# Two transformer blocks on one core: 38 of block 1's 56 input units computed as 19 pairs in seven half-size products each, with results through DRAM and the FFN's weight sums moved later

## The chip, the cores and the metric

The kernel runs on one core of a Trainium2 chip. The metric is the device time of one execution, in microseconds (us). The engines are TensorE (PE, matmuls; PEld is its weight load), VectorE (DVE), ScalarE (ACT), GpSimd (POOL) and SyncE (SP), which issues every DMA of this kernel from one in-order queue. Sixteen DMA engines move the data.

## What is computed

Two blocks on a sequence of 1024 rows of 1024 float32 numbers. Cut to what the change touches, block 1 is

```
h = rms_norm(x)
v_c, b_c, c_c, z_c, q, k, v, z_a, gate_a, gate_b = split(h @ w_in)     # 1024 columns each; k, v 256
y_c = b_c * conv3(c_c * v_c) * silu(z_c)          # causal depthwise convolution over the sequence
y_a = y_c @ w_conv_out
o   = sliding_window_attention(q, k, v, sinks) * silu(z_a)             # window 128, 16 heads of 64
y_b = o @ w_attn_out
x1  = x + (sigmoid(gate_a) * y_a + sigmoid(gate_b) * y_b) @ w_out
```

Block 2 is full causal attention with forget gates, a layer norm, a gated FFN of width 2816 with a convolution, a second layer norm and a gated embedding. It is not changed, but the sums of its FFN weights are made early, within block 1.

## The kernel before

All products keep float32 accuracy with three passes: an operand x is split into `hi` (ACT, line 84 or 81) and `lo` = x - hi (DVE, line 88 or 90), and each product is hi*hi + hi*lo + lo*hi. Operands that move through PE lie as two halves of 512 sequence positions (`XT.mov`). A *unit* is 128 output columns: a weight tile of 1024 x 128 (0.5 MB, rows of 512 bytes in DRAM, loaded by `spec_unit`, line 157) against both halves, 2 x 8 x 3 = 48 matmuls of 128x512 (`gemm_ws`, lines 181 to 183). `WQ` holds the list of weight tiles: `get` hands out one that is split, loads two ahead (`fetch`) and splits one ahead.

Block 1 goes in this order:

- `weave`: `attn1_stream` (32 items of the sliding attention, five stages in a software pipeline) and `beside` (8 convolution tiles of four input units each in `conv_stream`, then 3 units of gate b) take turns by an estimate of their matmul time, with the share RATIO = 0.68. The 16 tile buffers of h (`hT`) feed both. Results go to DRAM (`yc_d`, `o_d`, `gb_d`).
- `gates_b`: 5 more units of gate b; y_c comes back from DRAM and is split into `ycT`.
- `y_a`: 8 times a unit of gate a and a unit of w_conv_out. `z_a`: 8 units of z_a, times o from DRAM, into `ozT`. `y_b`: 8 units of w_attn_out, merged with gate b and y_a into `mT`. `w_out`: two halves of 512 columns; the first matmul group of a half needs all four weight tiles of that half.

All 56 *input units* (32 of the convolution, 16 gates, 8 z_a) are plain units with `hT`.

The FFN of block 2 is already computed by seven products of half size in place of eight (19 column tiles of the up projection, and the down projection). Its sums of weight blocks are made in block 1 by `Sums`, called `early`: each `early.step()` forms the sums of the pair loaded one call ago (four POOL additions of 128x512, line 381), stores them (four DMAs of 0.25 MB, `us_d` or `t_d`) and loads the next pair (two DMAs of 0.5 MB). There are 30 pairs, 19 of w_up (512-byte rows) and 11 of w_down. A call stands in 5 units of `gates_b`, in each of the 16 units of `y_a`, the 8 of `z_a` and the 8 of `y_b`.

`X7` and `up_products` are that FFN scheme: `X7.build` forms four combinations of quarter blocks of the moving operand, each with hi and lo; seven products of 12 matmuls accumulate in PSUM and are combined by ACT copies and DVE additions. Tiles of 4 KB per partition come from one pool of 46 buffers, tiles of 2 KB from a pool of 8, and there are 8 PSUM banks. The order on each engine is set by a scheduler at build time; the listings below show what it made. SP issues in its order, and a store waits there for its data, with every later DMA behind it.

Of the kernel before, what the change touches and what calls it, by code (L numbers as in the profile page):

```python
# [14 lines left out]
RATIO = 0.68  # L15
NG = 3
# [40 lines left out]
def tile_two_blocks(ctx: ExitStack, tc: tile.TileContext, I, out, dbg=None):  # L57
# [18 lines left out]
    def f(ap):  # L76
        return ap.bitcast(F32)
# [153 lines left out]
    for c in range(8):
        wq.add(spec_unit(w_in, C_G + c * 128))
        wq.add(spec_unit(I["w_conv_out"][0], c * 128))
    for c in range(8):
        wq.add(spec_unit(w_in, C_ZA + c * 128))
    for c in range(8):
        wq.add(spec_unit(I["w_attn_out"][0], c * 128))
    for ch in range(2):
        for kp in range(4):
            wq.add(spec_rows(I["w_out"][0], 2 * kp, 2, ch * 512, 512))  # L240
# [10 lines left out]
    add_v(0)  # L251
    for j in range(8):
        wq.add(spec_unit(w2i, j * 128))
        wq.add(spec_unit(w2i, 1024 + j * 128))
        if j % 2 == 1 and j < 7:
            add_v(j // 2 + 1)
    for ch in range(2):
        for kp in range(4):
# [107 lines left out]
    o_d = dr.tile([8, 128, 1024], F32, name="o_d")  # L366
    gb_d = dr.tile([8, 128, 1024], F32, name="gb_d")
# [64 lines left out]

    def conv_stream():
        for ct in range(8):
# [28 lines left out]
            cw = [pv1[:, 8 + 8 * k + ct:9 + 8 * k + ct] for k in range(3)]  # L463
            y = t4(name="y")
            dve.tensor_scalar(y, up, cw[2], None, op0=OP.mult)
            dve.scalar_tensor_tensor(out=y[:, 1:], in0=up[:, :1023], scalar=cw[1], in1=y[:, 1:],
                                     op0=OP.mult, op1=OP.add)
            dve.scalar_tensor_tensor(out=y[:, 2:], in0=up[:, :1022], scalar=cw[0], in1=y[:, 2:],
                                     op0=OP.mult, op1=OP.add)
# [174 lines left out]
    def yc_back(c):  # L644
        yr = t4(name="yr")
        sp.dma_start(out=yr, in_=yc_d[c])
        for hf in range(2):
            split_half(ycT, c, hf, yr[:, HS[hf]])

    def gates_b(c0, c1, back):  # L650
        for c in range(c0, c1):
            w = wq.get()
            if c >= NG:
                early.step()
            gt = t4(name="gt")
            for b in back(c):
                yc_back(b)
# [3 lines left out]
            sp.dma_start(out=gb_d[c], in_=gt)  # L661

    def y_a():
        for c in range(8):
            w = wq.get()
            early.step()
            gt = t4(name="gt")
            for hf in range(2):
                ps = yield from gemm_ws(w, hT, hf)
                act.activation(gt[:, HS[hf]], ps, AF.Sigmoid, bias=pv1[:, 32 + c:33 + c])  # L670
            w = wq.get()
            early.step()
            for hf in range(2):
# [4 lines left out]
    def z_a():  # L678
        for c in range(8):
            w = wq.get()  # L680
            early.step()
            orr = t4(name="orr")
            sp.dma_start(out=orr, in_=o_d[c])
            for hf in range(2):
                ps = yield from gemm_ws(w, hT, hf)
                s = t2(name="sz")
                act.activation(s, ps, AF.Silu)
                dve.tensor_tensor(out=s, in0=s, in1=orr[:, HS[hf]], op=OP.mult)
                split_half(ozT, c, hf, s)
# [488 lines left out]

# [3 lines left out]

    class X7:

        def __init__(self, x):
            self.x, self.T = x, {}  # L1190

        def build(self, kp, e=dve):
            b11, b21 = self.x.pair(0, kp), self.x.pair(0, 2 + kp)
            b12, b22 = self.x.pair(1, kp), self.x.pair(1, 2 + kp)

            def less(out, a, b):

                if isinstance(b, tuple):
                    tmp = t4((128, 2, 512), name="xs")
                    tt(e, tmp, f(a[1]), f(b[1]), OP.subtract)  # L1200
                    tt(e, out, f(a[0]), f(b[0]), OP.subtract)
                else:
                    tmp = f(a[1])
                    tt(e, out, f(a[0]), b, OP.subtract)
                tt(e, out, out, tmp, OP.add)

            def parts(i, src):
                h, l = t4((128, 2, 512), F32R, "xsh"), t4((128, 2, 512), F32R, "xsl")
                hi(h, src)
                lo(l, src, h)  # L1210
                self.T[i, kp] = h, l

            xt = {}
            for i, a, b in ((5, b12, b11), (6, b22, 5), (7, b22, b12), (4, b21, 6)):
                xt[i] = t4((128, 2, 512), name=f"xt{i}")
                less(xt[i], a, b if isinstance(b, tuple) else xt[b])
                yield
                parts(i, xt[i])
                yield

        def mov(self, i, q):
            if i in (1, 2, 3):
                return self.x.mov(q + (i > 1) * 4, int(i == 3))
            h, l = self.T[i, q // 2]
            return h[:, q % 2, :], l[:, q % 2, :]
# [39 lines left out]
    def product(ps, w, i, more=False):  # L1265
        for q in range(4):
            xh, xl = x7.mov(i, q)
            c = slice(q * 128, q * 128 + 128)
            st = q == 0 and not more
            pe.matmul(ps, lhsT=w[0][:, c], rhs=xh, start=st, stop=False, skip_group_check=more)  # L1270
            pe.matmul(ps, lhsT=w[0][:, c], rhs=xl, start=False, stop=False, skip_group_check=more)  # L1271
            pe.matmul(ps, lhsT=w[1][:, c], rhs=xh, start=False, stop=q == 3, skip_group_check=more)  # L1272

    def up_products(ct, gs, u):
        ps = {}

        def go(i, on=None):
            if i in (1, 6, 7, 4):
                op_split()
            if on is None:  # L1280
                ps[i] = bank()
            product(ps[on or i], ops.pop((ct, i)), i, more=on is not None)

        go(1)
        u1 = y2("u1")
        act.activation(u1, ps[1], AF.Copy)
        go(2)
        tt(dve, gs[:, HS[0]], ps[2], u1, OP.add)
        go(6, on=1)
        u2 = y2("u2")  # L1290
        act.activation(u2, ps[1], AF.Copy)
        go(5)
        u4 = y2("u4")
        tt(dve, u4, ps[5], u2, OP.add)
        go(7)
        tt(dve, u[:, HS[1]], ps[7], u4, OP.add)
        go(3)
        tt(dve, gs[:, HS[1]], ps[3], u4, OP.add)
        go(4, on=7)
        tt(dve, u[:, HS[0]], ps[7], u2, OP.add)  # L1300
# [264 lines left out]
```

## Time and profile before

| | us |
|---|---|
| median of 3 runs (lowest, highest) | 2537.41 (2536.05, 2537.45) |
| the profiled execution | 2536.48 |
| its span, first to last instruction | 2534.7 |
| PE busy | 2480.9 |
| DVE busy | 1457.0 |
| ACT busy | 1032.0 |
| POOL busy | 495.5 |

The terms of a sum are to be read against the profiled execution. Busy PE time is modelled up to the next matmul, so a gap in it is a wait of PE, while the share alone says little about the rate.

### The profile page before, as it was taken

To read this page: it belongs to the slowest core of one execution; us is meant where nothing else is said; L and a number is where in the kernel's file an instruction comes from. 1 tells how busy PE (TensorE), PEld (TensorE's weight loads), DVE (VectorE), ACT (ScalarE), POOL (GpSimd) and SP (SyncE) were. 2 spreads that over 40 slices of the span, in tenths; PEclk is the share of its full clock that TensorE was granted. 3 is DMA by queue.
4 is the path that set the end of the run, shared out by engine and by line. 5 is a ranking of instruction groups with operands and counts; after the bars stand their busy time and mean duration, and the time that the engine had idled before them with its cause. 6 is when DMAs were issued, how large, how long until landed. Compare 5 with 4: busy or idle time off the path is not lost. (4 is left out here: it accounts for less than half of the span.)

```text
span 2534.7 us, 33819 instructions
## 1 busy us (share of the span) xinstructions
PE 2480.9 (98%) x12558; PEld 2115.9 (83%) x12558; DVE 1457.0 (57%) x2859; ACT 1032.0 (41%) x1947; POOL 495.5 (20%) x446
## 2 busy tenths in 40 slices
PE   8999999999999999999999999999799999999999
PEld 7888888888888888888989898887677877888887
DVE  5566666755321355334666656568756566676873
ACT  4354444546221232124655656652333333354321
POOL 2000000000355561002232333414000000000331
PEclk9999999999999999999999999999999999999999
DMA  5121121212899997231111112523244444587512
GB/s 166 42 59 51 38 63 52 59 42 70 271 279 270 296 327 247 88 118 55 53 57 43 51 55 75 179 70 102 59 131 142 137 150 128 180 311 255 189 67 84
DMA packets 282480, 323.83 MB, mean 128 GB/s; under 512 B 23746, under 2 KB 197834, under 8 KB 282314
## 3 DMA queue, kind: packets, MB, share of 16 engines
q1 hardware_dynamic: 282314, 321.66, 39.3%
q8 instruction: 99, 1.62, 0.3%
q14 instruction: 67, 0.55, 0.1%
HBM read 233.20 MB, written 88.41 MB: 127 GB/s over the span
## 5 line engine op out<-in xcount | busy, mean ns | idle before, releaser
L181 PE MATMUL ps<-hTh,wh 128*128 128x512 f32 x896 | 353.0, 394 | 2.6 <-DVE hTl L90 2.5
L183 PE MATMUL ps<-hTh,wl 128*128 128x512 f32 x896 | 351.1, 392 | 0.0
L182 PE MATMUL ps<-hTl,wh 128*128 128x512 f32 x896 | 350.7, 391 | 0.0
L88 DVE TENSOR_TENSOR wl<-wraw,wh 128x1024 fp32r<-128x1024 f32 (+1 forms) x115 | 143.6, 1258 | 177.7 <-ACT wh L84 91.5
L84 ACT ACTIVATE wh<-wraw 128x1024 fp32r<-128x1024 f32 (+2 forms) x143 | 145.1, 1027 | 137.3 <-DMA us_d<-wraw 36.9
L183 PEld LDWEIGHTS ps<-hTh,wl 128*128 128x128 f32 x896 | 168.1, 188 | 35.7
L181 PEld LDWEIGHTS ps<-hTh,wh 128*128 128x128 f32 x896 | 168.4, 188 | 31.9 <-DVE hTl L90 3.1
L182 PEld LDWEIGHTS ps<-hTl,wh 128*128 128x128 f32 x896 | 168.4, 188 | 29.0
L1122 POOL TENSOR_SCALAR sm<-sm 128x1 f32<-128x1 f32 x16 | 11.6, 725 | 680.7 <-DVE sm L1120 680.7
L381 POOL TENSOR_TENSOR wraw<-wraw 128x512 f32<-128x512 f32 x76 | 105.8, 1393 | 162.2 <-DMA wraw<-in_ffn_w_up_dram 121.5
L1431 PE MATMUL ps<-dl,dh 128*128 128x512 f32 x308 | 119.9, 389 | 1.7 <-DVE dl L88 1.7
L1432 PE MATMUL ps<-dh,dl 128*128 128x512 f32 x308 | 119.9, 389 | 0.0
L88 POOL TENSOR_TENSOR wl<-wraw,wh 128x1024 fp32r<-128x1024 f32 (+2 forms) x28 | 65.1, 2331 | 267.1 <-ACT wh L84 245.1
L1430 PE MATMUL ps<-dh 128*128 128x512 f32 x308 | 117.1, 390 | 0.0
L88 DVE TENSOR_TENSOR phl<-ps,phl 128x512 fp32r<-128x512 f32 (+1 forms) x160 | 97.4, 633 | 31.6 <-ACT phl L84 30.3
L88 DVE TENSOR_TENSOR dl<-dr,dh 128x1024 fp32r<-128x1024 f32 x77 | 93.0, 1222 | 36.1 <-ACT dh L84 25.8
L321 POOL TENSOR_SCALAR sm<-sm 128x5 f32<-128x5 f32 (+1 forms) x40 | 10.5, 263 | 524.8 <-DVE sm L505 312.8
L84 ACT ACTIVATE dh<-dr 128x1024 fp32r<-128x1024 f32 x77 | 81.1, 1060 | 75.6 <-PE ps L1432 29.7
L181 PE MATMUL ps<-x1Th,wh 128*128 128x512 f32 x256 | 101.8, 398 | 1.4 <-DVE QB L90 1.4
L182 PE MATMUL ps<-x1Tl,wh 128*128 128x512 f32 x256 | 101.7, 397 | 0.0
L183 PE MATMUL ps<-x1Th,wl 128*128 128x512 f32 x256 | 100.6, 394 | 0.0
L897 POOL TENSOR_SCALAR p<-p,sm 128x640 f32<-128x640 f32 (+1 forms) x64 | 61.5, 964 | 177.5 <-DVE sm L896 126.3
(319 smaller groups left out, 6779.1 us busy)
## 6 DMA issues: line engine op xcount, KB each, us to landing
wraw<-in_ffn_w_up_dram SPq DMA_DIRECT2D x63, 512.0 KB, 6.1
wraw<-in_w_in_dram SPq DMA_DIRECT2D x56, 512.0 KB, 4.4
dr<-h_d SPq DMA_DIRECT2D x77, 256.0 KB, 3.7
us_d<-wraw SPq DMA_DIRECT2D x76, 256.0 KB, 3.2
wsr<-us_d SPq DMA_DIRECT2D x38, 512.0 KB, 6.1
wraw<-in_attn_w_in_dram SPq DMA_DIRECT2D x22, 512.0 KB, 3.8
h_d<-hs SPq DMA_DIRECT2D x44, 256.0 KB, 3.9
dr<-t_d SPq DMA_DIRECT2D x44, 256.0 KB, 5.4
```

Of the source, the lines that this page charges most:

```text
L84: act.activation(dst, src, AF.Copy, scale=1.0 if scale is None else scale)
L88: (eng or dve).tensor_tensor(out=dst, in0=src, in1=f(h), op=OP.subtract)
L181: pe.matmul(ps, lhsT=w[0][:, kt, :], rhs=xh, start=kt == 0, stop=False)
L182: pe.matmul(ps, lhsT=w[0][:, kt, :], rhs=xl, start=False, stop=False)
L183: pe.matmul(ps, lhsT=w[1][:, kt, :], rhs=xh, start=False, stop=kt == KT - 1)
L321: pool.tensor_scalar(v, ss, scale, eps, op0=OP.mult, op1=OP.add)
L381: e.tensor_tensor(out=out, in0=a, in1=b, op=op)
L897: pool.tensor_scalar(s["p"][q][:, :nk], s["p"][q][:, :nk], rc, 1.0, op0=OP.mult, op1=OP.mult)
L1122: pool.tensor_scalar(v, mv[:, 1:2], 1e-5, None, op0=OP.add)
L1430: pe.matmul(ps[j], lhsT=h[:, 0, c], rhs=h[:, 1, :], start=m == 0, stop=False)
L1431: pe.matmul(ps[j], lhsT=h[:, 0, c], rhs=l[:, 1, :], start=False, stop=False)
L1432: pe.matmul(ps[j], lhsT=l[:, 0, c], rhs=h[:, 1, :], start=False, stop=m == NM - 1)
```

## The change

Of the 56 input units, 18 stay plain: 3 convolution tiles (12 units, NCONV = 3), 1 unit of gate b beside the attention (NG = 1) and 5 behind it (NTR = 5). RATIO becomes 1.9, since the attention now has 13 units beside it, not 35. During the 5 units `X7.build` forms the combinations of h. The other 38 units become 19 pairs of neighbouring 128-column units, or of the v and c (and b and z) units of one convolution tile: `Pairs.run` calls `seven`, which computes both units of a pair in 7 x 12 = 84 matmuls in place of 96. The sums of a pair's weight blocks are made on DVE (`second`), the splits in `split`. Gate a and z_a results, which stayed in SBUF, now go through DRAM (`ga_d`, `oz_d`) and come back in `y_a`.

`y_a` then has only its 8 units of w_conv_out, and z_a is gone as a stage. The `early` calls stand 12 times in the 8 units of `y_a`, 12 times in the 8 of `y_b` and 8 times in `w_out`.

```diff
-RATIO = 0.68
-NG = 3
+RATIO = 1.9
+NCONV, NG, NTR = 3, 1, 5
...
+    def seven(x7, op, before, tmp, gs, u):
+        ps = {}
+        def go(i, on=None):
+            before(i)
+            if on is None:
+                ps[i] = bank()
+            product(x7, ps[on or i], op(i), i, more=on is not None)
+        go(1)
+        u1 = tmp("u1")
+        act.activation(u1, ps[1], AF.Copy)
+        yield
+        go(2)
+        tt(dve, gs[:, HS[0]], ps[2], u1, OP.add)
+        yield
+        go(6, on=1)
...
+        go(4, on=7)
+        tt(dve, u[:, HS[0]], ps[7], u2, OP.add)
...
+    class Pairs:
...
+        def split(self, n, src, i, j):
+            h, l = t4(dt=F32R, name="pwh"), t4(dt=F32R, name="pwl")
+            hi(h, src)
+            lo(l, src, h)
+            self.ops[n, i], self.ops[n, j] = [(h[:, c], l[:, c]) for c in HS]
...
+        def second(self, n):
...
+            tt(dve, x22, x21, x22, OP.add)
+            tt(dve, x21, x11, x21, OP.subtract)
+            tt(dve, x11, x22, x11, OP.subtract)
+            tt(dve, x12, x12, x11, OP.subtract)
...
+            def before(i):
+                if i == 1:
+                    self.split(n, self.raw[n][0], 6, 3)
+                elif i == 2:
+                    self.split(n, self.raw[n][1], 7, 5)
+                    del self.raw[n]
+                elif i == 6:
+                    self.load(n + 1)
+                elif i == 7:
+                    self.first(n + 1)
+                elif i == 3:
+                    self.second(n + 1)
...
     def y_a():
         for c in range(8):
             w = wq.get()
             early.step()
             gt = t4(name="gt")
+            sp.dma_start(out=gt, in_=ga_d[c])
             for hf in range(2):
-                ps = yield from gemm_ws(w, hT, hf)
-                act.activation(gt[:, HS[hf]], ps, AF.Sigmoid, bias=pv1[:, 32 + c:33 + c])
-            w = wq.get()
-            early.step()
-            for hf in range(2):
+                if c == 0 and hf == 0:
+                    for kp in range(4):
+                        back_load(yc_d, kp, 1)
+                        back_split(ycT)
+                if hf == 1:
+                    if c % 2:
+                        early.step()
+                    back_load(oz_d, c % 4, c // 4)
                 ps = yield from gemm_ws(w, ycT, hf)
                 dve.tensor_tensor(out=gt[:, HS[hf]], in0=ps, in1=gt[:, HS[hf]], op=OP.mult)
             sp.dma_start(out=ya_d[c], in_=gt)
...
     def y_b():
         for c in range(8):
             w = wq.get()
             early.step()
+            if c % 2:
+                early.step()
...
-    drain(gates_b(NG, 8, lambda c: range((c - NG) * 8 // (8 - NG), (c - NG + 1) * 8 // (8 - NG))))
+    build = chain(x7h.build(0), x7h.build(1))
+    for i, _ in enumerate(gates_b(NG, NG + NTR)):
+        next(build, None)
...
+    for c in range(NG + NTR, 8, 2):
+        gate_pair(c, 40, gb_d)
+    for ct in range(NCONV, 8):
+        conv_pairs(ct)
+    for c in range(0, 8, 2):
+        z_pair(c)
+    for c in range(0, 8, 2):
+        gate_pair(c, 32, ga_d, last_pair if c == 6 else None)
     drain(y_a())
-    drain(z_a())
     drain(y_b())
...
             for t in range(8):
+                if t % 2 == 0:
+                    early.step()
```

**SP in `y_a`, one round of the loop.** `wraw` are weight tiles (of a unit, or of a pair for the sums, from in_ffn_w_up), `us_d` stores of sums. Before, two units of PE work:

```order
L157 DMA wraw<-in_w_in_dram 128x8x128
L157 DMA wraw<-in_ffn_w_up_dram 128x8x128 x2
L157 DMA wraw<-in_w_conv_out_dram 128x8x128
L157 DMA wraw<-in_ffn_w_up_dram 128x8x128 x2
L414 DMA us_d<-wraw 128x512 x6
L676 DMA ya_d<-gt 128x1024
L414 DMA us_d<-wraw 128x512 x2
```

After, from the fourth weight of w_conv_out on, one unit of PE work up to the next `in_w_conv_out`:

```order
L157 DMA wraw<-in_w_conv_out_dram 128x8x128
L157 DMA wraw<-in_ffn_w_up_dram 128x8x128 x2
L855 DMA gt<-ga_d 128x1024
L157 DMA wraw<-in_ffn_w_up_dram 128x8x128 x2
L841 DMA br<-oz_d 128x2x512
L503 DMA us_d<-wraw 128x512 x2
L867 DMA ya_d<-gt 128x1024
L503 DMA us_d<-wraw 128x512 x4
L157 DMA wraw<-in_w_conv_out_dram 128x8x128
```

The two loads and four stores of a pair of sums stood once per unit; they now stand one to two times per unit, and gate a (`gt`) and o (`br`) come back between them.

**SP at the first weights of `w_out`.** `xr` are rows of x, `x_d` the stored x1, `gbr` and `yar` the operands of `y_b`. Before:

```order
L168 DMA wraw<-in_w_out_dram 128x2x512
L696 DMA gbr<-gb_d 128x1024
L698 DMA yar<-ya_d 128x1024
L168 DMA wraw<-in_w_out_dram 128x2x512 x3
L738 DMA x_d<-xr 128x512
L735 DMA xr<-in_x_dram 128x512
L738 DMA x_d<-xr 128x512
```

After, around the last of the four tiles that the first half needs, which is the first of the two in the fifth row (`wda` and `wdb` are a pair of w_down for the sums, `t_d` their stores):

```order
L490 DMA wda<-in_ffn_w_down_dram 128x1024
L490 DMA wdb<-in_ffn_w_down_dram 128x1024
L877 DMA gbr<-gb_d 128x1024
L879 DMA yar<-ya_d 128x1024
L168 DMA wraw<-in_w_out_dram 128x2x512 x2
L510 DMA t_d<-wda 128x512 x2
L510 DMA t_d<-wdb 128x512
L510 DMA t_d<-wda 128x512
L510 DMA t_d<-wdb 128x512
L510 DMA t_d<-wda 128x512
L510 DMA t_d<-wdb 128x512
L168 DMA wraw<-in_w_out_dram 128x2x512
```

Before, nothing but operands of `y_b` stood among these weights; now the loads and stores of the w_down sums do. From the first load for the sums in `y_a` to the fourth w_out tile, SP's list after the change holds 50 loads of 128x8x128 f32 (0.524 MB each, in 512-byte rows), 42 transfers of 128x1024 (0.524 MB), 16 loads of 128x2x512 (0.524 MB) and 88 stores of 128x512 (0.262 MB).

**DVE in the 5 plain units behind the attention.** `wl` is the lo part of a unit's weight, `xs`, `xt` and `xsl` are sums and lo parts of `X7.build`. Before:

```order
L88 TENSOR_TENSOR wl<-wraw,wh 128x1024 x2
L88 TENSOR_TENSOR ycTl<-yr,ycTh 128x512 x2
L88 TENSOR_TENSOR wl<-wraw,wh 128x1024
L88 TENSOR_TENSOR ycTl<-yr,ycTh 128x512 x4
L88 TENSOR_TENSOR wl<-wraw,wh 128x1024 x2
```

After, around one `wl`:

```order
L88 TENSOR_TENSOR xsl<-xt_4914,xsh 128x1024
L381 TENSOR_TENSOR xt_4935<-hTh,xt_4893 128x1024
L381 TENSOR_TENSOR xt_4935<-xt_4935,hTl 128x1024
L88 TENSOR_TENSOR xsl<-xt_4935,xsh 128x1024
L88 TENSOR_TENSOR wl<-wraw,wh 128x1024
L381 TENSOR_TENSOR xs<-hTl 128x1024
L381 TENSOR_TENSOR xt_4964<-hTh 128x1024
L381 TENSOR_TENSOR xt_4964<-xt_4964,xs 128x1024
L88 TENSOR_TENSOR xsl<-xt_4964,xsh 128x1024
L381 TENSOR_TENSOR xt_4985<-hTh,xt_4964 128x1024
L381 TENSOR_TENSOR xt_4985<-xt_4985,hTl 128x1024
L88 TENSOR_TENSOR xsl<-xt_4985,xsh 128x1024
```

Between two `wl` there were at most four half-tile operations; now fourteen whole-tile operations of the build stand on each side of one `wl`.

## Rows read from the trace of the kernel before

**Rows 1.** The page: span, and busy time of each engine.

```profile
span 2534.7 us, 33819 instructions
...
PE 2480.9 (98%) x12558; PEld 2115.9 (83%) x12558; DVE 1457.0 (57%) x2859; ACT 1032.0 (41%) x1947; POOL 495.5 (20%) x446
```

**Rows 2.** Windows: attention, `y_a`, `z_a`, `y_b`, `w_out`, and 200 us of plain units.

```profile
core 0: us, PE busy (x) PEld busy (x) DVE busy (x) ACT busy (x) POOL busy (x), PEclk, DMA share, GB/s
30.00:620.00 590.00, 587.09 (x3040) 512.51 (x3040) 376.48 (x1051) 285.29 (x687) 44.99 (x65) 1.00 0.18 52
...
700.00:880.00 180.00, 180.00 (x796) 149.06 (x795) 40.11 (x39) 33.59 (x43) 96.20 (x70) 1.00 0.92 280
880.00:957.00 77.00, 77.00 (x342) 63.75 (x341) 43.81 (x37) 24.82 (x37) 48.34 (x32) 1.00 0.92 330
957.00:1044.00 87.00, 87.00 (x385) 72.06 (x384) 46.05 (x58) 19.75 (x27) 3.75 (x3) 1.00 0.55 186
1044.00:1131.00 87.00, 87.00 (x410) 71.90 (x409) 26.20 (x49) 15.20 (x34) 4.22 (x3) 1.00 0.31 99
...
640.00:840.00 200.00, 200.00 (x884) 165.61 (x883) 49.11 (x46) 42.48 (x58) 98.01 (x72) 1.00 0.91 273
```

**Rows 3.** DVE groups, 90 to 600 us: the work of convolution units.

```profile
L88 DVE TENSOR_TENSOR wl<-wraw,wh 128x1024 fp32r<-128x1024 f32 x27 | 32.9, 1218 | 0.0
...
L462 DVE TENSOR_TENSOR up<-ps,v 128x512 f32<-128x512 f32 x14 | 9.6, 688 | 8.1 <-PE ps L183 7.9
L479 DVE TENSOR_TENSOR y<-y,sz 128x512 f32<-128x512 f32 x13 | 9.0, 693 | 24.2 <-ACT sz L478 24.1
...
L466 DVE SCALAR_TENSOR_TENSOR y<-up,pv,y 128x1023 f32<-128x1023 f32 x7 | 9.0, 1279 | 0.0
...
L465 DVE TENSOR_SCALAR y<-up,pv 128x1024 f32<-128x1024 f32 x7 | 5.3, 751 | 0.1
```

**Rows 4.** Windows: the busiest DVE beside the attention, and its end.

```profile
180.00:200.00 20.00, 20.00 (x108) 17.65 (x107) 18.24 (x45) 8.21 (x23) 1.89 (x4) 1.00 0.28 80
600.00:620.00 20.00, 17.72 (x89) 14.27 (x88) 16.62 (x48) 18.52 (x39) 0.00 (x0) 1.00 0.37 116
```

**Rows 5.** DVE groups, 1740 to 1835 us: `X7.build` in block 2.

```profile
L88 DVE TENSOR_TENSOR xsl<-xt,xsh 128x1024 fp32r<-128x1024 f32 x7 | 8.6, 1224 | 5.7 <-ACT xsh L84 5.7
...
L381 DVE TENSOR_TENSOR xt<-xt,xs 128x1024 f32<-128x1024 f32 x4 | 4.9, 1222 | 0.1
```

**Rows 6.** Waits of PE, 1740 to 1900 us: sum, times, longest.

```profile
PE ps L181 <- ACT wh L84: 12.7, 3, 11.9
```

**Rows 7.** Windows: PE and its granted clock (PEclk) around that wait.

```profile
1820.00:1825.00 5.00, 0.00 (x0) 0.00 (x0) 3.84 (x4) 2.95 (x3) 0.00 (x0) 0.50 0.00 0
1825.00:1830.00 5.00, 4.77 (x14) 3.84 (x15) 5.00 (x5) 0.18 (x1) 0.00 (x0) 0.63 0.00 0
```

**Rows 8.** Window: seven-product units of the FFN in block 2.

```profile
1900.00:2100.00 200.00, 196.73 (x862) 161.15 (x861) 123.76 (x143) 69.32 (x82) 0.00 (x0) 1.00 0.46 145
```

**Rows 9.** DMA, 740 to 860 us (`y_a`): packets by size, share of 16 engines.

```profile
DMA packets 41732, 32.82 MB, mean 273 GB/s; under 512 B 1350, under 2 KB 35079, under 8 KB 41724
...
q1 hardware_dynamic: 41724, 32.72, 90.8%
```

**Rows 10.** DMA, 2240 to 2290 us (down projection): packets by size, share.

```profile
DMA packets 9552, 19.52 MB, mean 390 GB/s; under 512 B 1063, under 2 KB 1063, under 8 KB 9549
...
q1 hardware_dynamic: 9549, 19.48, 104.5%
```

**Rows 11.** DMA, 640 to 964 us: packets by size, share.

```profile
DMA packets 93229, 94.89 MB, mean 293 GB/s; under 512 B 3878, under 2 KB 70438, under 8 KB 93208
...
q1 hardware_dynamic: 93208, 94.62, 91.0%
```

**Rows 12.** POOL groups, 640 to 964 us: sums of weight blocks.

```profile
L381 POOL TENSOR_TENSOR wraw<-wraw 128x512 f32<-128x512 f32 x76 | 105.8, 1393 | 162.2 <-DMA wraw<-in_ffn_w_up_dram 121.5 <-issue 16.0 <-DMA wraw<-in_w_conv_out_dram 10.4
L381 POOL TENSOR_TENSOR wdb<-wdb,wda 128x512 f32<-128x512 f32 x11 | 19.0, 1729 | 0.9
```

More of the change, by code (lines that the diff above doesn't have):

```diff
@@ L225, in tile_two_blocks @@
     wq = WQ(2)
-    for ct in range(8):
+    for ct in range(NCONV):
         for c in (C_V, C_C, C_B, C_Z):
             wq.add(spec_unit(w_in, c + ct * 128))
-    for c in range(8):
+    for c in range(NG + NTR):
         wq.add(spec_unit(w_in, C_G + D + c * 128))
[L231 to L240, printed above, removed]
     w2i = I["attn_w_in_2"][0]
@@ L381, in tt, with __init__, build, less @@
         e.tensor_tensor(out=out, in0=a, in1=b, op=op)
+    class X7:
+        def __init__(self, x):
+            self.x, self.T = x, {}
+        def build(self, kp, e=dve):
+            b11, b21 = self.x.pair(0, kp), self.x.pair(0, 2 + kp)
+            b12, b22 = self.x.pair(1, kp), self.x.pair(1, 2 + kp)
+            def less(out, a, b):
+                if isinstance(b, tuple):
+                    tmp = t4((128, 2, 512), name="xs")
+                    tt(e, tmp, f(a[1]), f(b[1]), OP.subtract)
+                    tt(e, out, f(a[0]), f(b[0]), OP.subtract)
+                else:
+                    tmp = f(a[1])
+                    tt(e, out, f(a[0]), b, OP.subtract)
+                tt(e, out, out, tmp, OP.add)
+            def parts(i, src):
+                h, l = t4((128, 2, 512), F32R, "xsh"), t4((128, 2, 512), F32R, "xsl")
+                hi(h, src)
+                lo(l, src, h)
+                self.T[i, kp] = h, l
+            xt = {}
+            for i, a, b in ((5, b12, b11), (6, b22, 5), (7, b22, b12), (4, b21, 6)):
+                xt[i] = t4((128, 2, 512), name=f"xt{i}")
+                less(xt[i], a, b if isinstance(b, tuple) else xt[b])
+                yield
+                parts(i, xt[i])
+                yield
+        def mov(self, i, q):
+            if i in (1, 2, 3):
+                return self.x.mov(q + (i > 1) * 4, int(i == 3))
+            h, l = self.T[i, q // 2]
+            return h[:, q % 2, :], l[:, q % 2, :]
@@ new lines, in product @@
+    def product(x7, ps, w, i, more=False):
+        for q in range(4):
+            xh, xl = x7.mov(i, q)
+            c = slice(q * 128, q * 128 + 128)
+            st = q == 0 and not more
+            pe.matmul(ps, lhsT=w[0][:, c], rhs=xh, start=st, stop=False, skip_group_check=more)
+            pe.matmul(ps, lhsT=w[0][:, c], rhs=xl, start=False, stop=False, skip_group_check=more)
+            pe.matmul(ps, lhsT=w[1][:, c], rhs=xh, start=False, stop=q == 3, skip_group_check=more)
+    def seven(x7, op, before, tmp, gs, u):
[8 more added lines that the diff above has]
+        act.activation(u1, ps[1], AF.Copy)
+        yield
+        go(2)
+        tt(dve, gs[:, HS[0]], ps[2], u1, OP.add)
+        yield
+        go(6, on=1)
+        u2 = tmp("u2")
+        act.activation(u2, ps[1], AF.Copy)
+        yield
+        go(5)
+        u4 = tmp("u4")
+        tt(dve, u4, ps[5], u2, OP.add)
+        yield
+        go(7)
+        tt(dve, u[:, HS[1]], ps[7], u4, OP.add)
+        yield
+        go(3)
+        tt(dve, gs[:, HS[1]], ps[3], u4, OP.add)
+        yield
+        go(4, on=7)
+        tt(dve, u[:, HS[0]], ps[7], u2, OP.add)
@@ L462, in conv_stream @@
                     dve.tensor_tensor(out=up[:, HS[hf]], in0=ps, in1=v[:, HS[hf]], op=OP.mult)
[L463 to L469, printed above, removed]
+            y = conv3(ct, up)
             w = wb or wq.get()
@@ new lines, in tile_two_blocks, with gate_pair @@
+    pairs = Pairs([(C_G + D + c * 128, C_G + D + c * 128 + 128) for c in range(NG + NTR, 8, 2)]
+                  + [(a + ct * 128, b + ct * 128) for ct in range(NCONV, 8) for a, b in ((C_V, C_C), (C_B, C_Z))]
+                  + [(C_ZA + c * 128, C_ZA + c * 128 + 128) for c in range(0, 8, 2)]
+                  + [(C_G + c * 128, C_G + c * 128 + 128) for c in range(0, 8, 2)])
+    def gate_pair(c, bias, dst, last=None):
+        for i, g in enumerate(pairs.run(last)):
+            act.activation(g, g, AF.Sigmoid, bias=pv1[:, bias + c + i:bias + c + i + 1])
+            sp.dma_start(out=dst[c + i], in_=g)
@@ new lines, in conv_pairs, with z_pair @@
+    def conv_pairs(ct):
+        v, up = pairs.run()
+        tt(dve, up, up, v, OP.mult)
+        y = conv3(ct, up, act)
+        b, z = pairs.run()
+        tt(dve, y, y, b, OP.mult)
+        act.activation(z, z, AF.Silu)
+        tt(dve, y, y, z, OP.mult)
+        sp.dma_start(out=yc_d[ct], in_=y)
+    def z_pair(c):
+        for i, z in enumerate(pairs.run()):
+            orr = t4(name="orr")
+            sp.dma_start(out=orr, in_=o_d[c + i])
+            act.activation(z, z, AF.Silu)
+            tt(dve, z, z, orr, OP.mult)
+            sp.dma_start(out=oz_d[c + i], in_=z)
@@ L663, in y_a, with back_load, back_split @@
+    back = deque()
+    def back_load(src, kp, hf):
+        r = t4((128, 2, 512), name="br")
+        sp.dma_start(out=r, in_=src[2 * kp:2 * kp + 2, :, HS[hf]].rearrange("c p n -> p c n"))
+        back.append((r, kp, hf))
+    def back_split(dst):
+        r, kp, hf = back.popleft()
+        h, l = dst.pair(hf, kp)
+        hi(h, r)
+        lo(l, r, h)
     def y_a():
@@ L676, in y_a @@
             sp.dma_start(out=ya_d[c], in_=gt)
[L678 to L689, printed above, removed]
+            back_split(ozT)
     def y_b():
@@ L706, in beside, with last_pair @@
         yield from cs
-        yield from gates_b(0, NG, lambda c: ())
+        yield from gates_b(0, NG)
     weave(attn1_stream(), beside(), RATIO)
-    drain(gates_b(NG, 8, lambda c: range((c - NG) * 8 // (8 - NG), (c - NG + 1) * 8 // (8 - NG))))
+    build = chain(x7h.build(0), x7h.build(1))
+    for i, _ in enumerate(gates_b(NG, NG + NTR)):
+        next(build, None)
+        if i == 8 * NTR - 16:
+            pairs.load(0)
+        elif i == 8 * NTR - 8:
+            pairs.first(0)
+        elif i == 8 * NTR - 4:
+            pairs.second(0)
+    drain(build)
+    def last_pair(i):
+        if i == 6:
+            for kp in range(4):
+                back_load(yc_d, kp, 0)
+            add_later()
+            wq.fetch(1)
+        elif i in (7, 3):
+            back_split(ycT)
+            back_split(ycT)
+        elif i == 4:
+            wq.split()
+    for c in range(NG + NTR, 8, 2):
[6 more added lines that the diff above has]
+        gate_pair(c, 32, ga_d, last_pair if c == 6 else None)
     drain(y_a())
-    drain(z_a())
     drain(y_b())
@@ L1185, in y2 @@
         return yp.tile([128, 512], F32, name=name, tag="y2")
[L1187 to L1225, printed above, removed]
     x7 = X7(x2T)
@@ L1263, in op_split, with before @@
         op_load()
[L1265 to L1272, printed above, removed]
     def up_products(ct, gs, u):
-        ps = {}
-        def go(i, on=None):
+        def before(i):
             if i in (1, 6, 7, 4):
                 op_split()
[L1280 to L1300, printed above, removed]
+        drain(seven(x7, lambda i: ops.pop((ct, i)), before, y2, gs, u))
     def ffn_conv(ct, gs):
```

86 lines of the change are left out of this document (63 added, 23 removed).

## The prediction

> **What bounds the kernel now.** I read the page first: PE is busy in 2480.9 of 2534.7 us [rows 1], but that share says only that PE seldom waits. The windows by stage come next. In all five stages of block 1 that the change touches, PE is busy in at least 587 of 590 us and its granted clock is full [rows 2], so what a matmul less is worth can be read there: 200 us hold 884 matmuls of plain units, 0.2262 us each. A unit is 48 of them, 10.86 us. The other columns tell what stands close behind PE. Beside the attention it is DVE, with 376 of 590 us. In `y_a` and `z_a` it is the DMA engines: their share is 0.92 in both, at 280 and 330 GB/s, while PE still doesn't wait [rows 2]. After that the share falls to 0.55 in `y_b` and 0.31 in `w_out`. So block 1 has a stretch in which the queue is nearly full, and it is full of the sums of the FFN weights: 30 pairs, each 1.05 MB in and 1.05 MB out, 63 of the 94.9 MB that move between 640 and 964 us [rows 11].
>
> **PE's work.** 19 pairs of 84 matmuls take the place of 38 units of 48: 1596 for 1824, 228 fewer. All are 128x512, and nothing else of PE's work changes. 228 x 0.2262 = 51.6 us less. This is the whole gain; every other term is a wait that PE did not have.
>
> **The attention with less beside it.** 22 units leave the stretch from 30 to 620 us, which gives PE 590 - 22 x 10.86 = 351 us of work there. DVE loses the work of five convolution tiles. By the groups of DVE [rows 3] one tile costs 4 weight splits of 1.218, six half-tile products of 0.69 and 0.75 + 2 x 1.28 for the convolution, 12.3 us; five, and two gate splits, are 64 us. So DVE keeps 376 - 64 = 312 us for 351 us of PE, 89%. Nearest rows: DVE was at 18.2 of 20 us once with no wait of PE, and at 16.6 of 20 at the attention's end, where ACT was at 18.5 and PE lost 2.3 us [rows 4]. The bounds are 0 (DVE carries 89% throughout) and 40 us (it manages 80%, 312 / 0.8 = 391 us). I take **10**, near the lower end, since PSUM's 8 banks let PE run ahead.
>
> **The build of the sums of h.** `X7.build` costs 20 sums of 1.222 and 8 lo parts of 1.224 us [rows 5], 34 us of DVE in the 54 us of five units. The listing shows fourteen of these on each side of one `wl`: 17 us between two weights, where PE consumes one every 10.86. The same build in block 2 stands in the same way among plain units, and PE there waited 11.9 us for a weight [rows 6], its clock falling to 0.50 and coming back over the next stretch [rows 7]. Bounds 0 (the weights were split ahead) and 14 (that wait and its slow matmuls, 5 us at 0.63 of the clock costing about 2 us). I take **12**: the pattern is the same.
>
> **The pairs themselves.** A pair takes PE 84 x 0.2262 = 19.0 us. DVE has 3 lo parts of 1.218, one of half size, four sums and four PSUM additions of 0.69, 9.9 us, and up to 3.2 us more for a convolution's share; ACT has less. The seven-product units of block 2, with the same chain, lose 3.3 us of PE in 200 [rows 8], so the 361 us of pairs lose about **5** (bounds 0 and 10). The DRAM round trips of gate a and o lie here at about 2 MB a pair, 110 GB/s, and cost nothing: in the seven-product units of block 2 the queue took 145 GB/s at a share of 0.46 [rows 8]. Without that cover they would join the queue of the next term.
>
> **The sums, moved into less time.** This term decides. Before, the 30 pairs went through 31 units from 620 to 957 us, and the queue was at 0.91 [rows 11]. Now they go through `y_a`, `y_b` and the start of `w_out`, and `y_a` has only 8 units; gate a and o come back there too. `w_out` cannot start before the fourth of its weight tiles, and SP's list fixes what stands ahead of it (every DMA is on one queue): from the start of `y_a` 50 loads of 0.524 MB in 512-byte rows, 26.2 MB, and 42 + 16 transfers of 0.524 MB and 88 of 0.262 MB in longer rows, 53.5 MB; 79.7 MB together. PE's work up to there is 16 units, 174 us, so PE would need 458 GB/s.
>
> What the queue can carry is read from two rows. Long rows: 390 GB/s over 50 us at a share of 1.045, that is, full [rows 10]. For 512-byte rows I take `y_a`: packets under 2 KB less those under 512 B are 33729, 17.3 MB of 32.8; the queue was busy for 0.908 x 120 = 109 us, the other 15.5 MB take 40 us at 390, and so 17.3 MB took 69 us, 250 GB/s [rows 9]. The two rates give 66560 x 512 B = 34.1 MB in 136 us and 60.8 MB in 156 for 640 to 964 us, 292 us, where the share says 0.91 x 324 = 295 [rows 11]; so they hold. Then 79.7 MB take 26.2 / 0.250 + 53.5 / 0.390 = 105 + 137 = 242 us. The last tile's split adds about 2 us. Bounds: all at 390 GB/s, 204 us; or a queue that is kept only as full as in rows 11, 242 / 0.91 = 266 us. It will not be kept full, since SP stops at each store until POOL has made its sum and at each `ya_d` until DVE has it, with the next weight behind; I take the middle, 254 us. PE then waits 254 + 2 - 174 = 82 us in `y_a`, `y_b` and before `w_out`, and about 4 us more for matmuls at the lower clock after the gaps, as in [rows 7]: **86** (bounds 32 and 98). What follows, some 23 MB, needs 60 us under `w_out`'s 87 us of matmuls and costs nothing.
>
> The Trainium skill, "DMA: Bandwidth & Descriptors", Specifications, gives 512 B as the least transfer at which a DMA engine reaches line rate; by that the 26.2 MB would go as fast as the rest, and the term would be its lower bound of 32. The trace disagrees: 512-byte rows took 69 us for 17.3 MB.
>
> **Sum.** Profiled execution 2536.48 us: -51.6 + 10 + 12 + 5 + 86 = +61.4, 2597.9. The median of the runs is 0.9 us above it, so **2599 us**. All lower bounds: -51.6 + 32 = -20, 2518; all upper: -51.6 + 40 + 14 + 10 + 98 = +110, 2648.
>
> **Rivals.** (1) *The queue carries it.* If the mix goes at 390 GB/s and the attention, the build and the pairs cost nothing, the result is 2518 us, faster. It decides at one point: the 79.7 MB must be through in less than 174 + 51.6 - 2 = 224 us, 356 GB/s. For it: stretches of 390 GB/s exist [rows 10]. Against it: those had no 512-byte rows, and the term ignores three other costs. Chance 0.11; within 0.2% (5 us, about what a measurement of this kernel can tell from no change) 0.06. (2) *All rows at 390 GB/s, the other terms as above*: 204 + 2 + 4 - 174 = 36, 2536.5 - 51.6 + 27 + 36 = 2548. Chance 0.15. The rule of the Trainium skill above ("DMA: Bandwidth & Descriptors", Specifications) stands behind this one. (3) *SP stands longer at the stores.* POOL needs 4 x 1.39 us for a pair of sums, 22 pairs before `w_out` are 123 us, or 152 at the 1.73 of its slower rows [rows 12]; that is below 254, so POOL is no bound, but a late sum holds up the weight behind it. At a share of 0.8 the queue takes 303 us: 2647. Chance 0.13. (4) *DVE bounds the attention*: +40 in place of +10, 2629. Chance 0.13. Near my sum: 0.42.
>
> The range from 2520 to 2655 leaves out about half of case 1 and the tail of case 3. Faster 0.11, same 0.06, slower 0.83.
>
> **What would show it.** Right: in the changed kernel's windows the share of the DMA engines is at 0.9 or above from the start of `y_a` to `w_out`, at 310 to 340 GB/s; PE is busy in about two thirds of that stretch, in gaps that end with a weight's split that waited for a DMA; the longest stands before `w_out`'s first matmul; PEclk falls there and nowhere else but in the five plain units behind the attention, where one gap of some 10 us ends on `wh` or `wl`. The pairs run at 19.0 us each. Wrong: if `y_a` and `y_b` take 174 us, the queue carries more than any row shows, and the result is 1 or 2% below mine; if PE waits mostly before 400 us, it is DVE beside the attention.

## The result, and the profile after

2638.8 us (median of 4 runs, 2637.2 to 2640.3) against 2536.9 before: ratio 1.040, 95% interval 1.038 to 1.042. The profiled execution's span went from 2534.7 to 2638.5 us, 103.8 more, inside the range and on the side that was forecast; 40 us above the point.

The page of the changed kernel, its first part (as [rows 1]):

```profile
span 2638.5 us, 33658 instructions
...
PE 2477.2 (94%) x12330; PEld 2099.0 (80%) x12330; DVE 1627.2 (62%) x3052; ACT 1068.7 (41%) x1976; POOL 491.5 (19%) x446
```

PE has 228 instructions less and is busy almost as long as before: its matmuls were slower in stretches, and a stretched matmul counts as busy. So the stages are read from windows; those of the pairs, `y_a`, `y_b` and `w_out` are cut at the first matmul that reads the stage's operand. They are, in order: the attention; its end with the five plain units; the pairs; `y_a`; `y_b`; `w_out` (columns as in [rows 2]).

```profile
30.00:400.00 370.00, 359.00 (x2005) 323.90 (x2004) 291.56 (x911) 213.78 (x582) 42.85 (x63) 1.00 0.15 43
400.00:500.00 100.00, 80.34 (x339) 65.65 (x338) 67.96 (x118) 43.94 (x82) 1.36 (x2) 0.86 0.20 63
502.00:883.00 381.00, 363.93 (x1569) 297.68 (x1568) 228.65 (x276) 121.72 (x143) 0.00 (x0) 0.98 0.33 100
884.00:1016.00 132.00, 100.60 (x384) 77.92 (x382) 37.87 (x34) 20.43 (x20) 56.68 (x40) 0.86 0.95 299
1016.00:1134.00 118.00, 96.34 (x382) 76.73 (x383) 61.24 (x54) 18.49 (x25) 71.41 (x49) 0.90 1.00 329
1134.00:1241.00 107.00, 97.29 (x439) 79.21 (x438) 38.21 (x58) 18.82 (x39) 47.54 (x36) 0.94 0.78 277
```

`y_b` is the plainest: the same 8 units, 385 matmuls, took 87 us with the DMA engines' share at 0.55 [rows 2], and now 118 at 1.00. Waits of PE from 884 to 1136 us (sum, times, longest):

```profile
PE ps L181 <- ACT wh L84: 25.2, 9, 6.2
PE ps L181 <- ACT ycTh L84: 12.7, 1, 12.7
PE ps L181 <- ACT ozTh L84: 8.1, 1, 8.1
PE ps L183 <- DVE wl L88: 7.1, 7, 1.4
```

PE waits for the split of a weight, or for the operands that came back from DRAM; behind both stands a transfer. The queue from 884 to 1134 us (as [rows 9]):

```profile
DMA packets 77035, 78.22 MB, mean 313 GB/s; under 512 B 3085, under 2 KB 57332, under 8 KB 77024
...
q1 hardware_dynamic: 77024, 78.08, 97.5%
```

### The profile page after: what moved, and what is told of

Same layout as the page of the kernel before. It is cut to its first block, busy times and chain, and to the rows that moved or that the text cites. A ratio compares the mean times of both kernels' runs of the same rounds, so it can differ in the third digit from the quotient of the medians.

```text
span 2638.5 us, 33658 instructions
## 1 busy us (share of the span) xinstructions
PE 2477.2 (94%) x12330; PEld 2099.0 (80%) x12330; DVE 1627.2 (62%) x3052; ACT 1068.7 (41%) x1976; POOL 491.5 (19%) x446
## 5 line engine op out<-in xcount | busy, mean ns | idle before, releaser
L381 DVE TENSOR_TENSOR u<-ps,u 128x512 f32<-128x512 f32 x76 | 52.4, 690 | 159.6 <-PE ps L436 123.2
L84 ACT ACTIVATE wh<-wraw 128x1024 fp32r<-128x1024 f32 (+3 forms) x105 | 105.5, 1016 | 71.2 <-DMA wraw<-in_w_in_dram 16.8
L181 PE MATMUL ps<-hTh,wh 128*128 128x512 f32 x288 | 116.4, 405 | 8.4 <-ACT wh L84 5.6
L88 DVE TENSOR_TENSOR wl<-wraw,wh 128x1024 fp32r<-128x1024 f32 (+1 forms) x77 | 98.2, 1283 | 38.7 <-ACT wh L84 32.2
L182 PE MATMUL ps<-hTl,wh 128*128 128x512 f32 x288 | 115.6, 401 | 0.0
L183 PE MATMUL ps<-hTh,wl 128*128 128x512 f32 x288 | 115.2, 402 | 0.0
L434 PE MATMUL ps<-xsh,pwh 128*128 128x512 f32 x228 | 92.2, 404 | 17.1 <-ACT pwh L84 17.0
L84 ACT ACTIVATE phl<-ps 128x512 fp32r<-128x512 f32 (+1 forms) x160 | 83.3, 553 | 27.8 <-PE ps L1120 21.6
L436 PE MATMUL ps<-xsh,wol 128*128 128x512 f32 x228 | 87.0, 394 | 5.9 <-DVE wol L88 5.9
L435 PE MATMUL ps<-xsl,pwh 128*128 128x512 f32 x228 | 91.2, 400 | 0.0
```

The lines of the kernel that those rows point to most:

```text
L84: act.activation(dst, src, AF.Copy, scale=1.0 if scale is None else scale)
L88: (eng or dve).tensor_tensor(out=dst, in0=src, in1=f(h), op=OP.subtract)
L181: pe.matmul(ps, lhsT=w[0][:, kt, :], rhs=xh, start=kt == 0, stop=False)
L182: pe.matmul(ps, lhsT=w[0][:, kt, :], rhs=xl, start=False, stop=False)
L183: pe.matmul(ps, lhsT=w[1][:, kt, :], rhs=xh, start=False, stop=kt == KT - 1)
```

## The experiments

Each is a single run, beside the kernel before at 2536 to 2538 us, unless more runs are named. The four runs of the changed kernel spread over 3 us, and those of combo, combo5 and combo8 over 3 to 8, so a single difference of some 8 us or less says little. A stage's length is from the first matmul on its operand to the first on the next; `w_out` ends with its last matmul. The pairs are counted from the first product that reads a sum of h.

| | total | pairs | `y_a` | `y_b` | `w_out` |
|---|---|---|---|---|---|
| kernel before | 2536.9 | | | 87.1 | 93.1 |
| changed kernel | 2638.8 | 382.1 | 132.3 | 118.5 | 106.9 |
| no_sums | 2559.4 | 381.0 | 99.1 | 87.0 | 93.1 |
| sums_raw | 2625.3 | 381.6 | 130.9 | 110.5 | 99.8 |
| sums_own_queue | 2646.4 | 381.0 | 123.5 | 136.3 | 104.6 |
| sums_in_pairs | 2571.0 | 386.1 | 105.5 | 87.0 | 93.1 |
| conv_dve | 2622.9 | 369.6 | 128.1 | 114.6 | 107.6 |
| build_spread | 2627.7 | 386.4 | 129.9 | 113.2 | 108.2 |
| build_pool | 2643.0 | 383.1 | 132.9 | 114.8 | 107.6 |
| conv8 | 2614.0 | | 128.7 | 115.4 | 107.0 |
| combo | 2555.7 | 380.3 | 105.1 | 87.0 | 93.2 |
| combo5 | 2558.1 | | 119.9 | 87.1 | 93.1 |
| combo8 | 2577.3 | | 123.2 | 99.3 | 93.1 |
| before_late | 2576.9 | | | 116.0 | 106.0 |

**no_sums.** The theory: the sums, squeezed into fewer units, fill the one DMA queue. The rival: the new round trips do it.

```diff
-            self.todo = deque([("up", ct) for ct in range(NPLAIN, NCT)] + [("down", m) for m in range(NM)])
+            self.todo = deque()
...
-            sp.dma_start(out=r.rearrange("p (k c) -> p k c", c=512), in_=us_d[ct][:, i:i + 2, :])
+            sp.dma_start(out=r.rearrange("p (k c) -> p k c", c=512), in_=wdn[ct * 128:ct * 128 + 128, :].rearrange("p (k c) -> p k c", c=512))
...
-        return t_d[{5: 0, 6: 1, 7: 2, 4: 3}[i]][m]
+        return wdn[m * 128:m * 128 + 128, HS[0]]
```

> Leaves out all FFN weight sums with their loads and stores; the FFN reads plain weight blocks of the same size and row length in their place, so that its own time stays. Theory (the full DMA queue): y_a and y_b need 174 us of PE in place of 251, w_out about 94 in place of 107; the run is about 90 us shorter, 2540 to 2560 us. Rival (the round trips of gate a, o and y_c or the missing buffers hold up y_a, whatever the queue): less than 30 us shorter, above 2610.

79 us shorter, as the theory had it. `y_b` and `w_out` have their lengths of before to 0.1 us. The sums cost 33.2 + 31.5 + 13.8 = 78.5 us in the three stages. What is left in `y_a`, 99.1 for 86.9 us of matmuls, is the rival's share, 12 us; its one wait is for the second half of y_c (window and wait of `y_a` in this run):

```profile
882.00:981.00 99.00, 90.18 (x385) 73.89 (x384) 35.43 (x39) 22.51 (x22) 0.00 (x0) 0.95 0.67 226
...
PE ps L181 <- ACT ycTh L84: 8.8, 1, 8.8
```

**sums_raw.** The eight POOL additions in `Sums.step` are taken out, as

```diff
-                    tt(pool, x22, x21, x22, OP.add)
...
-                    tt(pool, x21, x21, x22, OP.subtract)
```

> Keeps every load and store of the sums and leaves out the POOL additions between them: the raw blocks are stored. Theory (bytes of the queue): the 79.7 MB ahead of w_out stay, so from the start of y_a to w_out it takes 235 to 250 us (251 now), 2620 to 2640 us in all. Rival (SP standing at stores for POOL, 51 us in the trace): the stretch falls by 40 us or more, 2600 us or less.

13.5 us less in all, 16.5 in the three stages. In the changed kernel SP stood 51 us in all at stores of up sums (L503) for POOL; without POOL's additions the queue only got fuller (window of `y_b` in this run):

```profile
1015.00:1125.00 110.00, 96.19 (x383) 76.90 (x384) 39.55 (x55) 17.66 (x24) 0.00 (x0) 0.92 1.06 357
```

So a fifth of the 78.5 us goes with POOL's additions, by SP's stands for them or by what they do to DVE; the run does not part the two. The rest stays with the transfers and SP's other stops.

**sums_own_queue.** In `Sums`, `sp.dma_start` becomes `pool.dma_start`.

> The loads and stores of the sums are issued from POOL's own queue, so that no weight stands behind them on SP; bytes and additions are the same. Theory in its strict form (the DMA engines' rate binds PE through the order of one queue): the operands of y_a and y_b are 30 MB and need about 190 GB/s beside the sums, which two queues share; PE's waits from y_a to w_out fall from 91 to 15 to 40 us, 2565 to 2590 us, and the sums end later. Rival (the engines are full and every transfer is late, whichever queue it is in): above 2615 us.

No gain: the time is on the rival's side, 8 us above the changed kernel. `y_b` took 136 us though no weight stood behind a sum in SP's order any more, so taking the weights out of that order is not enough. Windows of `y_a` and `y_b` in this run:

```profile
880.00:1004.00 124.00, 90.81 (x387) 73.46 (x386) 38.85 (x34) 20.50 (x20) 80.97 (x85) 0.89 0.96 304
1004.00:1140.00 136.00, 98.01 (x385) 76.59 (x384) 59.27 (x55) 17.83 (x24) 102.14 (x115) 0.87 0.84 279
```

The rival's reason, that the engines are full, fits `y_a` with a share of 0.96, but not `y_b` with 0.84. POOL, now the issuer, stood at loads for tiles that PE and DVE still held (29 and 16 us in its waits), and SP stood 56 us in its own at stores of `ya_d` for gate a, with the next weights behind. So buffers and what is left of SP's order may have a part; how much was not tried.

**sums_in_pairs.**

```diff
+                elif i == 5:
+                    early.step()
                 elif i == 7:
                     self.first(n + 1)
...
-            early.step()
-            if c % 2:
+            if c < 6:
                 early.step()
```

and fewer calls in `y_a` and `w_out`.

> One call of the sums in each of the 19 pairs, 2 in y_a, 6 in y_b, 4 in w_out (31 in all, as needed). Theory: the queue has room in the pairs (share 0.2 to 0.6 there) and is no bound in y_a and y_b then: 75 to 90 us shorter, 2550 to 2565 us. Rival: the four buffers of each pair of sums and POOL's additions beside DVE's slow the pairs by 20 us or more and give part back: above 2575.

68 us less, short of the 75 that were expected. `y_b` and `w_out` are free; the pairs became 4 us longer, and `y_a` still waited 15.9 us for y_c.

**before_late.** One part of the change alone, on the kernel before.

```diff
-            if c >= NG:
-                early.step()
...
             early.step()
+            if c % 2:
+                early.step()
             gt = t4(name="gbr")
```

> The kernel before with one part of the change alone: the calls of the sums leave gates_b and y_a and stand 12 times in z_a, 12 in y_b and 8 in w_out, as late and as dense as in the changed kernel; no pairs. Theory: the same queue, with 10 MB less beside it (o is read, gate a is not): 26 MB at 250 and some 43 MB at 390 GB/s are 215 us for 174 us of PE, and SP's stops come on top: 45 to 65 us slower, 2582 to 2602 us. Rival (the queue is a bound only together with the pairs' round trips through DRAM): less than 25 us slower.

40 us slower, 5 below the expected range, with no pair in the kernel. So dense sums cost time without the pairs' round trips, but only half of the 78.5 us: `y_b` lost 29 and `w_out` 13, nearly what no_sums gave back there, while `z_a`, with as many calls as `y_b` and a queue as full, kept its 88 us. What the sums cost in `y_a` (33 us) has no counterpart here. Windows of `z_a` and `y_b`:

```profile
868.00:956.00 88.00, 88.00 (x390) 72.86 (x389) 48.14 (x36) 24.92 (x38) 56.96 (x36) 1.00 0.98 292
956.00:1072.00 116.00, 94.52 (x385) 75.60 (x384) 58.00 (x54) 17.57 (x25) 68.34 (x48) 0.91 1.03 338
```

The rest of the forecast had PE's own losses before `y_a` at 27 us; they are 66 (below). Four runs concern these.

**conv_dve.**

```diff
-        y = conv3(ct, up, act)
+        y = conv3(ct, up)
```

> The first step of the convolution in the pairs goes from ACT to DVE (the convolution itself is unchanged). Theory: the gaps of PE in the pairs come from ACT's in-order queue, where that step waits up to 6.7 us for DVE's product and three weight splits stand behind it; without it the pairs (382 us from the first use of a sum of h to y_a) come down by 15 to 20 us, 2618 to 2625 us in all. Rival (DVE is late in any case, or the DMA of the weights): the gaps stay, within 5 us of 2638.

Pairs 12.5 us shorter (15 to 20 were expected), in all 16. In the changed kernel ACT, in order, waits for `pb` and holds three splits of the next pair (timeline, ACT):

```profile
539.48 1.15 ACT L81 ACTIVATE y<-pb,pv 128x1024 f32<-128x1024 f32 x1 [4.38 <-DVE pb L381]
540.53 2.94 ACT L84 ACTIVATE pwh<-wraw 128x1024 fp32r<-128x1024 f32 x3
```

PE's waits in the pairs there, and with the edit:

```profile
PE ps L434 <- ACT pwh L84: 17.0, 8, 4.0
```

```profile
PE ps L436 <- DVE pwl L88: 8.5, 5, 1.9
```

**build_spread.**

```diff
-        next(build, None)
+        if i >= 8 and i % 2 == 0:
+            next(build, None)
```

> The 16 steps of the build of the sums of h start one plain unit later and come at every second instead of every matmul step (32 matmul steps instead of 16). Theory: the gap of PE at 400 to 480 us comes from the build standing ahead of the attention's last DVE work and of the weight splits; it goes, with the lower clock that it causes, 20 to 30 us: 2608 to 2620 us. Rival (the attention's end is held by its own chain on DVE and ACT): less than 8 us, above 2630.

11 us, half of what was expected; the first product on a sum of h came 10.3 us earlier. The gap at the weight split at 460 us went (PE 20.0 of 20); the one at the attention's end shrank from 8.8 to 5.2 us and stayed. Waits of PE in the changed kernel, 410 to 505 us, and the first of them in this run, 400 to 500 us:

```profile
PE ps L683 <- DVE p L672: 11.3, 2, 8.8
PE ps L181 <- ACT wh L84: 5.6, 1, 5.6
```

```profile
PE ps L683 <- DVE p L672: 7.7, 2, 5.2
```

Windows of this run:

```profile
400.00:420.00 20.00, 14.35 (x70) 11.74 (x68) 16.84 (x61) 16.46 (x42) 1.36 (x2) 0.74 0.25 80
...
460.00:480.00 20.00, 20.00 (x90) 16.57 (x89) 14.79 (x13) 5.86 (x7) 0.00 (x0) 1.00 0.36 106
```

So the build was one cause of two. In this run no operation of the build is on DVE before 438 us, and PE still stands at the attention's end: its last items are a chain through DVE and ACT, with no matmul of a plain unit between them from 411 to 428 us.

**build_pool.** `x7h.build(0, pool)` and `x7h.build(1, pool)`.

> The 20 sums of the build are made on POOL, which has nothing else to do there; the lo parts stay on DVE. Theory: 24 us less of DVE, the attention's last work is not held, 10 to 25 us less: 2613 to 2628 us. Rival: POOL takes about 2.5 us for one (two of its half tiles at 1.39 and less), 50 us in all, so the sums are late for the first pair and the gap only moves: above 2630 us.

The rival: no gain, 4 us longer. POOL took 2.4 to 2.8 us for a sum (2.79 the longest group), where 1.22 was DVE's [rows 5], and the first product on a sum came 2.5 us later.

**conv8.**

```diff
-RATIO = 1.9
-NCONV, NG, NTR = 3, 1, 5
+RATIO = 0.67
+NCONV, NG, NTR = 8, 1, 5
```

> All 8 convolution tiles stay plain beside the attention (NCONV 8, share 0.67), so 9 pairs are left: PE has 120 matmuls more, 27 us. If the waits beside the attention and at the end of it come from too little PE work beside DVE's, the 11 us of gaps before 400 us and most of the 30 us at the sums of h go, and the 20 us of gaps in the convolution pairs go too: 2590 to 2605 us. If the sums of h alone hold up DVE there, that gap stays: 2625 to 2640 us. The stretch of y_a and y_b stays at 251 us in both.

2614 us: 25 less, though PE has 27 us more of matmuls, so some 52 us of waits left with the ten convolution pairs, 47 of them ahead of `y_a`. That lies between the two expectations, whose times stand for 61 to 76 us and for 26 to 41 us of waits less. PE was busy in 584 of 590 us from 30 to 620. The wait at the attention's end (9.7 us) stayed, as the second theory had it.

**combo, combo5, combo8** (five runs each, combo8 four). combo is sums_in_pairs, conv_dve and build_spread, with `y_a` in the order

```diff
+        for c, hf in [(0, 0), (1, 0), (0, 1), (1, 1)] + [(c, hf) for c in range(2, 8) for hf in range(2)]:
```

> Four edits together: sums in the pairs (2571), the convolution's first step on DVE (15 us), the build spread over 32 matmul steps (11 us), and y_a taking the first halves of two units before the second halves, so that the second half of y_c has 5 us more to arrive (its wait is 9 to 16 us in the runs so far; 8 us less). If the four causes are separate, they add: 2571 - 15 - 11 - 8 = 2537, within 5 us of the kernel before. If they cover each other, above 2550.

> As the four edits together, with 5 in place of 3 convolution tiles beside the attention (share 1.1) and 15 pairs: 48 matmuls more, 11 us, against part of the 11 us of waits beside the attention and of some 20 at its end. If these waits come from too little PE work beside DVE's, 2525 to 2537 us, at or below the four edits; if the end of the attention waits for the build alone, 2540 to 2550.

> As the four edits together, with all 8 convolution tiles plain beside the attention (share 0.67) and 9 pairs: 120 matmuls more than with 3 tiles, 27 us, and no wait beside the attention. The pairs save 24 us against the kernel before; the end of the attention and the build cost 10 to 20: 2522 to 2537 us. Above 2540 the seven products pay nothing in this block even where they stand alone.

combo is 2555.7 us, ratio 1.0074 to before (1.0061 to 1.0086); combo5 2558.1, 1.0085 (1.0071 to 1.0099); combo8 2577.3, 1.0161 (1.0147 to 1.0175). None beats the kernel before, and the single gains don't add: 2537 was expected of combo. It fell short in two places. `y_a` took 105.1 us, as it did without its new order (105.5 in sums_in_pairs): its wait for y_c fell from 15.9 to 3.1 us, but 6.6 us of waits for weights came, and its matmuls were busy for 94.8 us, not 89.6. And the pairs took 380 us, where conv_dve had 370; sums_in_pairs and build_spread had each lengthened them by 4. One reason is in DVE's rows: the additions of the sums on POOL now run beside DVE. DVE groups of the pairs, 510 to 860 us, in conv_dve:

```profile
L88 DVE TENSOR_TENSOR pwl<-wraw,pwh 128x1024 fp32r<-128x1024 f32 x53 | 63.9, 1220 | 18.5 <-ACT pwh L84 18.5
...
L381 DVE TENSOR_TENSOR pa<-ps,u 128x512 f32<-128x512 f32 x36 | 24.8, 688 | 3.3 <-PE ps L436 2.6
```

and in combo, with POOL's group:

```profile
L88 DVE TENSOR_TENSOR pwl<-wraw,pwh 128x1024 fp32r<-128x1024 f32 x53 | 81.1, 1544 | 20.7 <-ACT pwh L84 20.7
...
L381 DVE TENSOR_TENSOR pa<-ps,u 128x512 f32<-128x512 f32 x35 | 24.0, 686 | 1.2 <-PE ps L436 0.5
```

```profile
L381 POOL TENSOR_TENSOR wraw<-wraw 128x512 f32<-128x512 f32 x68 | 115.2, 1694 | 236.8 <-DMA wraw<-in_ffn_w_up_dram 232.8
```

The lo parts, whose operands all lie in SBUF, went from 1.220 to 1.544 us; additions with one operand in PSUM kept 0.69. The Trainium skill, "GPSIMD Engine Reference", Specifications, says that GpSimd's way into SBUF is shared with VectorE, with contention for DVE instructions that have two SBUF inputs; the two groups agree with it.

combo5 and combo8 have fewer pairs to hold the sums, so more calls stand in `y_a` (6 and 8 for 2; combo8 has 8 in `y_b` too): combo5 reached `y_a` 12.6 us sooner than combo, and `y_a` took 119.9 us, 14.8 more. Their expectations, which priced only the attention, missed that. The same kernels with those calls elsewhere were not run.

## Why the prediction was right, and where its sizes were off

By stages, with the sums of no_sums set apart:

| term | predicted | measured |
|---|---|---|
| 228 matmuls less | -51.6 | -51.6 (by count) |
| attention and build | 10 + 12 | 40 |
| pairs | 5 | 26.5 |
| the queue, and what stands in `y_a` | 86 | 91 |
| block 2 | 0 | -2 |
| sum | 61 | 104 |

The measured 40 is what remains when the others are taken from 103.8. The 26.5 is 382.1 less the matmuls of that window, 19 x 19.0 - 24 x 0.2262 = 355.6 us: 24 matmuls of the first pair come before its first product on a sum.

**The queue** was right in mechanism and nearly in size. It carried 78.2 MB in 250 us where 79.7 in 254 were forecast, at 0.975 of its time and 313 GB/s. The two rates hold for the new mix: 57332 - 3085 packets, taken as 512 B each, are 27.8 MB, the other 50.4 MB take 129 us at 390 GB/s, and of the 244 us in which the queue was busy 115 are left for the short rows, 242 GB/s where 250 was read. no_sums shows that the sums cause 78.5 us of the 91, and before_late that they cost 40 us without pairs. Not foreseen were the 12 us for y_c's second half inside the 91, and the order of loss. Up to `w_out`'s first matmul the loss was 77 us, not 86: PE stood idle for 53 (82 were forecast), and its matmuls were busy for 197 us instead of 173, at a mean granted clock of 0.86 and 0.90, where 4 us were forecast for the lower clock. Some 14 us came after that matmul, where I had nothing: `w_out` began before all its weights were there and then stood for one (waits of PE, 1134 to 1242 us):

```profile
PE ps L196 <- ACT wh L84: 8.5, 1, 8.5
```

The longest wait of the stretch stood not before `w_out`, where the prediction had it, but at y_c's second half in `y_a` (12.7 us, above). So it is partly luck that 86 and 91 agree so well. Rival 1 (the queue carries it) and rival 2 (all rows at 390 GB/s) fall with the 313 GB/s. Rival 3, SP's stands for POOL, is a part: at most 16.5 us by sums_raw. The Trainium skill, "DMA: Bandwidth & Descriptors", Specifications, has line rate from 512 B on; the 242 GB/s here speak against it once more.

**The attention** was mis-sized. From 30 to 400 us it cost what was said, 11 us of idle PE (370 - 359.0). But its last items, from 400 to 432 us, cost some 20 more, and of the 29 us that were lost between 400 and 500 (40 - 11) they are the larger part. The step that failed was to take the end at the row of the kernel before, where PE lost 2.3 us [rows 4]: there matmuls of plain units stood between the last items, and here none did from 411 to 432 us. PE stood 8.8 us in one gap, and after it ran at the lower of its two clocks, 1.2 GHz (window of the changed kernel):

```profile
424.00:430.00 6.00, 2.91 (x10) 2.44 (x11) 5.88 (x12) 1.06 (x1) 0.00 (x0) 0.50 0.00 0
```

With some 31 us in all it lies inside its bounds of 0 and 40, nearer to the +40 of rival 4 than to the 10 that were taken.

**The build** came out near its 12: some 9 us were lost in the five plain units, 5.6 of them in one wait for a weight, and some 3 at the attention's end, where DVE did three operations of the build ahead of the last normalisation. build_spread gave 10 of them back. The split of the 40 between these two terms is an estimate, from the counts of matmuls in the two windows and from build_spread.

**The pairs** were mis-sized, 26.5 for 5. The row that I took [rows 8] has ACT's first convolution step before the split of the next weights too, so the chain was taken to be the same. It is not: the FFN's step needs only `gs`, which is complete one product before the pair's end, while here it needs the product of both results, which DVE can form only after the pair's last matmul. That is read from the kernel. What a run shows is that conv_dve gave back 12.5 of the 21.5 us; the other 9 stay open. A pair took 20.4 us on average, not the 19.0 of the prediction's sign.

## What to carry to other kernels

Work that is free where it stands, and is moved to another stage, has to be priced as bytes over the time of that stage: here 80 MB for 174 us of PE decided, and the saved matmuls could not. Rates of the queue are best taken apart by row length from two stretches of the same trace, and checked on a third. A step that waits long in an in-order queue of ACT or DVE costs what stands behind it, and more than its gap if PE's clock falls; and work that is put beside another engine's may slow it, so single gains measured apart need not add.

## What was not expected of the hardware

Gaps of PE cost more than their length: the mean granted clock went from 0.996 to 0.973 of full speed, and stood at 0.74 from 400 to 440 us and 0.86 to 0.94 in the last three stages; in `y_a` and `y_b` the slower matmuls took 24 us beside 53 us of gaps. Sums issued from POOL's own queue were no faster for PE than in SP's (2646 and 2639 us). POOL's two-input additions and DVE's were both slower beside each other in the pairs of combo: 1.39 [rows 12] to 1.69, and 1.22 to 1.54 us. A full queue does not always stop PE: `z_a` of before_late ran at a share of 0.98 without a wait.
